# Moving the block merges and the two recurrences of a chunked DeltaNet layer, and putting three half projections between the last recurrence's steps

## The chip, the core and the metric

One core of a Trainium2 chip runs the whole program. The metric is the device time of one execution in microseconds (us), as the median of several runs. The profile shows one execution, with the work of every engine: PE is the matmul engine, DVE, ACT and POOL work on vectors, and SP issues the loads.

## The reference

Two decoder layers over 512 positions of width 1024, in float32. Layer 0 mixes tokens with a gated DeltaNet (8 heads of 128), layer 1 with a convolution module; each then attends to a memory of 256 rows and applies a squared-ReLU MLP. The change lies in the DeltaNet of layer 0 and at the seam to the attention behind it:

```python
proj = h @ w_in                       # q, k, v, z, and two gates for each head
qkv = silu(causal_depthwise_conv(qkv, w_conv))
# by chunk: (I + L) is unit lower triangular, L = strict(k_beta k^T * decay)
sol = triangular_solve(a_mat, rhs)    # u, w
def step(state, inp):                 # over the chunks, in order
    v_new = uc - wc @ state
    o = qd @ state + ai @ v_new
    state = state * exp(gl) + kd^T @ v_new
o = o * rsqrt(mean(o * o) + eps) * out_norm * silu(z)
h = h + o.reshape(B, S, 1024) @ w_out
```

## The kernel before

Activations are held transposed, as eight tiles of 128 channels by 512 positions. A weight tile and an activation tile are each split into a high and a low part (`wh`, `wl` and so on), and a product is three matmuls (`mm3`, lines 220 to 222). So a projection of one output tile is 24 matmuls, and half a projection, over four of the eight input tiles, is 12.

The weights of a unit are loaded by SP into one of three `raw` buffers (line 193), copied to `wh` by ACT (line 204) and subtracted to `wl` by DVE (line 72). Three pairs of `wh` and `wl` exist, and `wnext` asks for the splits of the next two units when a unit begins.

The DeltaNet works in chunks of 128 positions, four of them, and in two groups of four heads. Its order is written out by hand: `mains` is a list of units of PE work, most of them half a projection (`halves`), and `S.at(i, rank, f)` puts a side step behind unit `i`, the lower ranks first. Units 4 to 33 are the projections k, q, z and v of group 0, units 34 to 65 those of group 1, and units 66 to 81 the keys and values of the memory for the attention (`kv_unit`; the first eight give K, with 256 columns for each matmul, the last eight V). A scheduler then orders each engine's queue from that list, by priorities and by when it expects an operand; each engine works through its own queue strictly in that order.

The side steps that the change moves:

- The merge. The triangular matrix of each chunk is inverted in blocks of 32. DVE eliminates within the blocks (`fs_steps`, with tiles `FT`, `X`, `fst`) and ends with two transposes, to `TB` and `UB` (`fs_end`, lines 517 and 518, behind units 29 and 58). Then, for each head, `mg_a` copies four blocks of `TB` to `x` on ACT (line 537) and four of `UB` to `u` on POOL (line 538); `mg_w` multiplies (line 546) and copies to `w` (line 548); `mg_y`, three times, multiplies (line 558), copies to `y` (line 561) and adds to `u`. `MG` is the unit where this starts for each group; the second group's heads start up to two units before it.
- The recurrence. `rec(gq, c, step)`: for each chunk `c` three steps in three units. Step 0 multiplies keys and state (`kS`, line 618) and forms `r` on DVE; step 1 multiplies with the inverse (`vn`, line 630) and scales to `vnd` and `vn` on DVE; step 2 updates the state (`S`, line 641) and gives the outputs (`qS`, line 652, and `o`, line 658). `o_gate` follows in the third unit behind, and `o_norm` (root on ACT at line 680, scaling of the four `z` tiles on POOL and DVE) one unit after the last gate. `REC` is the first unit for each group.
- `head_out` transposes a head's gated output (`ogT`, line 691) and splits it into `oh` and `ol` for the output projection `do`. Heads 0 to 3 are done at units `HO` = 76 to 79.
- `load_x` loads the residual input again, behind unit `REC[1] + 6`.

Other steps in these stretches: each conv head is evicted by DVE (`cv`, line 72), scaled by ACT (lines 415 and 419), added by POOL (`cva`) or DVE (line 75), and passed through Silu by ACT (line 426). `k2` and `q2` (lines 440 to 466) form the Gram products of a head. The memory's norm runs beside it: squares on ACT (line 710), sums on POOL (`msq`), a product on PE (`mssq`, line 719), the root on ACT, scaling on POOL (`mem`) and the split into `mh` and `ml` on ACT and DVE (`mem_gain`), which the K units read.

After the list, the output projection is written out: first halves of units 0 and 1 over heads 0 to 3, then `head_out` for heads 4 to 7, then the second halves, and units 2 to 7 whole. `do_ev` adds the residual and starts the attention's norm.

Of the kernel before, what the change touches and what calls it, by code (L numbers as in the profile page):

```python
# [40 lines left out]
def tile_trunk(ctx, tc, xT, memT, prm_d, adt_d, bdw_d, w_ab, w_kq, w_v, w_z, w_dno, w_pw1, w_pw2,  # L41
# [13 lines left out]
    def nm(s):  # L55
        cnt[0] += 1
        return f"{s}_{cnt[0]}"

    def slot(dt=F32, s="u", shape=(P, NT)):
        return up.tile(list(shape), dt, tag="u", name=nm(s))  # L60

    def psum(s="ps"):
        return psp.tile([P, NT], F32, tag="ps", name=nm(s))
# [7 lines left out]
    def tt(e, o, a, b, op):  # L71
        e.tensor_tensor(out=o, in0=a, in1=b, op=op)  # L72
# [24 lines left out]
    def load_x():  # L97
        r = []
        for t in range(KT):
            h = slot(s="x")  # L100
            nc.sync.dma_start(out=h, in_=xT[t * P:(t + 1) * P, :])
            r.append(h)
        return r
# [84 lines left out]
    def wload():  # L188
        u = ws["load"]
        key, hf = order[u]  # L190
        ws["load"] += 1
        raw = wp.tile([P, 1024], F32, tag="raw", name=nm("raw"), bufs=NRAW)
        nc.sync.dma_start(out=raw, in_=srcs[key][:, hf * 1024:(hf + 1) * 1024])
        ws["raw"][u] = raw

    def wsplit():
        u = ws["split"]
        ws["split"] += 1
        while ws["load"] <= u:
            wload()  # L200
        raw = ws["raw"].pop(u)
        h = wp.tile([P, 1024], F32R, tag="wh", name=nm("wh"), bufs=NW)
        lo = wp.tile([P, 1024], F32R, tag="wl", name=nm("wl"), bufs=NW)
        act.copy(h, raw)  # L204
        tt(dve, lo, raw, h.bitcast(F32), ALU.subtract)
        ws["hl"][u] = (h, lo)

    def wnext(key, hf):
        i = ws["next"]
        assert order[i] == (key, hf), (order[i], key, hf)  # L210
        while ws["load"] < min(i + NRAW + 2, len(order)):
            wload()
        while ws["split"] < min(i + (NW if i else 1), len(order)):
            wsplit()
        ws["next"] += 1
        return ws["hl"].pop(i)

    def mm3(ps, wk, xk, first, last):
        (wh, wl), (xh, xl) = wk, xk
        pe.matmul(ps, wh, xh, start=first, stop=False)  # L220
        pe.matmul(ps, wh, xl, start=False, stop=False)  # L221
        pe.matmul(ps, wl, xh, start=False, stop=last)  # L222

    def wk(w, k):
        c = slice(k * P, (k + 1) * P)
        return w[0][:, c], w[1][:, c]

    def proj(w, xs, ps, k0=0, k1=KT):
        for k in range(k0, k1):
            mm3(ps, wk(w, k), xs[k], k == 0, k == KT - 1)  # L230
# [31 lines left out]
    def run(mains, sides):  # L262

        last = max(int(k[0]) for k in sides) + 1
        for i in range(max(len(mains), last)):
            if i < len(mains):
                mains[i]()
            for k in sorted(k for k in sides if k[0] == i):
                for f in sides[k]:
                    f()  # L270
# [476 lines left out]
    def kv_unit(layer, u):  # L747
        if u == 0:
            KV[layer] = ([], {})
        K, V = KV[layer]  # L750
        if u < 8:
            if u % 2 == 0:
                mem["ps"] = psum("K")
            hf = u % 2
            proj(wnext(("K", layer, u // 2), hf), mem["xs"], mem["ps"][:, hf * 256:(hf + 1) * 256])
            if hf == 1:
                K.append(split(mem["ps"], "K"))
        else:
            v = u - 8
            g, q, hf = v // 4, v // 2 % 2, v % 2  # L760
            if v % 4 == 0:
                mem["ps"] = [psum("V") for _ in range(2)]
            proj_moving(wnext(("V", layer, g * 2 + q), hf), hf, q, mem["xs"], mem["ps"])
            if v % 4 == 3:
                for mt in range(2):
                    V[mt, g] = split(mem["ps"][mt], "V")
# [338 lines left out]
    mains, S = [], Sides()  # L1105
# [27 lines left out]
    for u in range(16):  # L1133
        mains.append(lambda u=u: kv_unit(0, u))

    def squares(t0, t1):
        for t in range(t0, t1):
            n0.square(xin[t])

    S.at(0, 0, squares, 0, SQ0)  # L1140
    S.at(0, 3, wsplit)
    S.at(0, 2, squares, SQ0, 8)
    S.at(T_STAT, 0, n0.stat)
    S.at(T_STAT + 2, 0, n0.spread)
# [20 lines left out]
    for gq in range(2):  # L1165
# [6 lines left out]
        for i in range(4):  # L1172
            h = 4 * gq + i
            m = MG[gq] + i * MSTEP[gq] // 2
            S.at(m, 1, D.mg_a, h)
# [6 lines left out]
        for c in range(4):  # L1182
            for step in range(3):
                S.at(REC[gq] + n, 0, D.rec, gq, c, step)
                n += 1
            S.at(REC[gq] + n, 5, D.o_gate, gq, c)
        S.at(REC[gq] + n + 1, 1, D.o_norm, gq)
    S.at(MEM, 7, mem_load)
# [2 lines left out]
    S.at(MEM + 9, 3, mem_stat)  # L1191
    S.at(at["kv"] - MGAIN, 6, mem_gain, 0, 0)
    S.at(at["kv"] - MGAIN + 1, 6, mem_gain, 0, 1)
    os_, xres = [], []
    for i in range(4):
        S.at(HO + i, 6, lambda i=i: os_.append(D.head_out(i)))
    S.at(REC[1] + 6, 8, lambda: xres.extend(load_x()))
    run(mains, S)
# [4 lines left out]
    def do_ev(m, ps):  # L1203
        hn = slot(s="h")
        tt(dve, hn, ps, xres[m], ALU.add)
        h.append(hn)
        n1.add(m, hn)

    def do_w(m):
        return wnext(("do", m // 2), m % 2), psum("do")  # L1210

    w0, p0 = do_w(0)
    proj(w0, os_, p0, 0, 4)
    w1, p1 = do_w(1)
    proj(w1, os_, p1, 0, 4)
    for i in range(4, 8):
        os_.append(D.head_out(i))
    proj(w0, os_, p0, 4, 8)
    do_ev(0, p0)
    proj(w1, os_, p1, 4, 8)  # L1220
    do_ev(1, p1)
    for m in range(2, 8):
        w, ps = do_w(m)
        proj(w, os_, ps)
        do_ev(m, ps)
    n2 = Norm("mlp_norm0")
    h = xattn(0, n1, h, n2)
# [85 lines left out]
Q2 = (16, 18, 20, 21, 46, 48, 48, 51)  # L1313
FS = ((20, 9), (50, 8))
MSTEP = (0, -1)
MG = (32, 63)
V2 = (4, 3)
MGAIN = 4
HO = 76
REC = (39, 68)  # L1320
MEM = 53
MLP_ORDER = [("up", 0), ("up", 1), ("dn", 0), ("up", 2), ("dn", 1), ("up", 3), ("dn", 2), ("dn", 3)]
TAP_RATE = 1.5
# [95 lines left out]
```

## Time and profile before

| | us |
|---|---|
| median of 3 runs (1599.11 to 1601.5) | 1600.11 |
| the profiled execution | 1601.85 |
| its span, from first to last instruction | 1599.7 |
| PE busy | 1542.7 |
| DVE busy | 924.3 |
| ACT busy | 660.6 |
| POOL busy | 275.9 |

The mean granted clock of PE is 0.983. PE's busy time is 96% of the span. The DeltaNet ends at some 380 us; the rest of the span is attention, MLP and the second layer. A queue's wait is seen in the idle time in front of an instruction: the profile gives it in brackets, with the instruction that ended it.

### The profile page before, as it was taken

How to read it: one execution, taken by the hardware profiler on the slowest of the kernel's cores; microseconds unless marked ns; L12 is line 12 of the kernel's file. 1: busy time of each engine (PE TensorE's matmuls, PEld its weight loads, DVE VectorE, ACT ScalarE, POOL GpSimd, SP SyncE). 2: the span in 40 equal slices, each digit the busy share in tenths (PEclk: the TensorE clock that was granted, in tenths of full speed). 3: DMA queues.
4: the chain of work that ended last, by engine and by line, in shares of the span. 5: the costliest groups of instructions: out<-in, count | busy, mean ns of one | idle time of the engine just before them, and what ended most of it. 6: DMA issues, size and time to landing. Idle time of an engine off the chain costs nothing.

```text
span 1599.7 us, 20039 instructions
## 1 busy us (share of the span) xinstructions
PE 1542.7 (96%) x7864; PEld 1307.5 (82%) x7864; DVE 924.3 (58%) x1373; ACT 660.6 (41%) x1011; POOL 275.9 (17%) x314
## 2 busy tenths in 40 slices
PE   9998997899999999999999999799999999999997
PEld 6777885798888888888888889788888888888897
DVE  6886878576455444343436599974545443444443
ACT  6656573745444433232314321173434442322332
POOL 1526334502111100000111308102012000000002
PEclk9999999899999999999999999899999999999999
DMA  5221112153211232232232421253213222322321
GB/s 178 67 72 60 53 51 95 53 172 110 94 63 64 92 105 93 94 104 92 94 104 93 141 90 47 85 160 106 79 40 99 95 97 92 105 93 93 104 93 53
DMA packets 47614, 147.09 MB, mean 92 GB/s; under 512 B 6304, under 2 KB 11040, under 8 KB 47520
## 3 DMA queue, kind: packets, MB, share of 16 engines
q1 hardware_dynamic: 47520, 145.81, 27.6%
q8 instruction: 62, 1.02, 0.3%
q14 instruction: 32, 0.26, 0.1%
HBM read 142.38 MB, written 2.10 MB: 90 GB/s over the span
## 4 chain that ended last, share of the span: by engine, by line
PE 89%; DVE 3%; POOL 3%; ACT 2%; issue 1%; DMA 0%; DVEq 0%; SPq 0%; POOLq 0%; ACTq 0%
PE dn L222 7%; PE dn L220 7%; PE dn L221 7%; PE up L220 7%; PE up L222 7%; PE up L221 7%; PE pw L220 3%; PE pw L221 3%; PE pw L222 3%; PE q L220 2%; PE xo L221 2%; PE q L221 2%; PE q L222 2%; PE cv L1024 2%; PE xo L220 2%; PE xo L222 2%
## 5 line engine op out<-in xcount | busy, mean ns | idle before, releaser
L204 ACT CAST wh<-raw 128x1024 fp32r<-128x1024 f32 x248 | 260.5, 1051 | 717.5 <-PE dn L221 191.4
L72 DVE TENSOR_TENSOR wl<-raw,wh 128x1024 fp32r<-128x1024 f32 x248 | 314.2, 1268 | 127.4 <-ACT wh L204 121.5
L220 PE MATMUL up<-xh,wh 128*128 128x512 f32 x512 | 200.2, 391 | 0.0
L222 PE MATMUL up<-xh,wl 128*128 128x512 f32 x512 | 199.2, 389 | 0.0
L221 PE MATMUL up<-xl,wh 128*128 128x512 f32 x512 | 199.2, 389 | 0.0
L220 PE MATMUL dn<-uh,wh 128*128 128x512 f32 x448 | 174.3, 389 | 0.0
L221 PE MATMUL dn<-ul,wh 128*128 128x512 f32 x448 | 174.3, 389 | 0.0
L222 PE MATMUL dn<-uh,wl 128*128 128x512 f32 x448 | 174.3, 389 | 0.0
L72 DVE TENSOR_TENSOR h<-dn,h 128x512 f32<-128x512 f32 x56 | 41.8, 747 | 170.4 <-PE dn L222 170.4
L75 DVE SCALAR_TENSOR_TENSOR rl<-up,rb 128x512 f32<-128x512 f32 x64 | 44.2, 691 | 156.9 <-PE up L222 156.9
L221 PEld LDWEIGHTS up<-xl,wh 128*128 128x128 f32 x512 | 96.1, 188 | 20.3 <-issue 0.5
L220 PEld LDWEIGHTS up<-xh,wh 128*128 128x128 f32 x512 | 96.1, 188 | 20.1 <-issue 0.5
L222 PEld LDWEIGHTS up<-xh,wl 128*128 128x128 f32 x512 | 96.1, 188 | 20.1
L72 POOL TENSOR_TENSOR tap<-ident,prm 128x512 f32<-128x512 f32 x45 | 61.0, 1388 | 278.6 <-PE up L222 263.8
L221 PEld LDWEIGHTS dn<-ul,wh 128*128 128x128 f32 x448 | 84.1, 188 | 17.6
L222 PEld LDWEIGHTS dn<-uh,wl 128*128 128x128 f32 x448 | 84.1, 188 | 17.5
L220 PEld LDWEIGHTS dn<-uh,wh 128*128 128x128 f32 x448 | 84.1, 188 | 17.3
L72 POOL TENSOR_TENSOR sq<-sq,sq 128x512 f32<-128x512 f32 x30 | 49.9, 1664 | 255.4 <-ACT sq L295 167.7
L75 DVE SCALAR_TENSOR_TENSOR ca<-xg,prm,ca 128x384 f32<-128x384 f32 (+3 forms) x159 | 88.2, 607 | 0.3
L220 PE MATMUL h<-xh,wh 128*128 128x512 f32 x192 | 77.5, 403 | 1.3 <-ACT xh L288 1.3
L221 PE MATMUL h<-xl,wh 128*128 128x512 f32 x192 | 75.5, 393 | 0.6 <-DVE xl L75 0.6
L222 PE MATMUL h<-xh,wl 128*128 128x512 f32 x192 | 75.2, 392 | 0.0
(320 smaller groups left out, 3204.4 us busy)
## 6 DMA issues: line engine op xcount, KB each, us to landing
raw<-w_up SPq DMA_DIRECT2D x64, 512.0 KB, 3.5
raw<-w_dn SPq DMA_DIRECT2D x64, 512.0 KB, 3.5
raw<-w_pw SPq DMA_DIRECT2D x24, 512.0 KB, 3.7
raw<-w_kq SPq DMA_DIRECT2D x16, 512.0 KB, 3.6
raw<-w_k SPq DMA_DIRECT2D x16, 512.0 KB, 3.7
raw<-w_vv SPq DMA_DIRECT2D x16, 512.0 KB, 4.0
raw<-w_q SPq DMA_DIRECT2D x16, 512.0 KB, 3.6
raw<-w_o SPq DMA_DIRECT2D x16, 512.0 KB, 3.6
```

Of the source, the lines that this page charges most:

```text
L72: e.tensor_tensor(out=o, in0=a, in1=b, op=op)
L75: dve.scalar_tensor_tensor(out=o, in0=a, scalar=s, in1=b, op0=op0, op1=op1)
L204: act.copy(h, raw)
L220: pe.matmul(ps, wh, xh, start=first, stop=False)
L221: pe.matmul(ps, wh, xl, start=False, stop=False)
L222: pe.matmul(ps, wl, xh, start=False, stop=last)
L1024: pe.matmul(o, x, TAPS[m][2 * j + u // 4][:, (u % 4) * P:(u % 4 + 1) * P], start=u == 0, stop=False)
```

## The change

The merges start two and three units later (`MG`), the recurrences two and four (`REC`), and with `REC[1]` also `load_x`. The first halves of the output projection's units 0, 1 and 2 become units 82 to 84 of the list, so that the last steps of the second recurrence stand between them; the list's end moves with the last gate and `o_norm`. Afterwards the second halves of these three units follow on `head_out` of heads 4 to 7.

```diff
+    os_, xres, first = [], [], []
+
+    def do_first(m):
+        first.append((wnext(("do", m // 2), m % 2), psum("do")))
+        proj(first[m][0], os_, first[m][1], 0, 4)
+
+    for m in range(NDO):
+        mains.append(lambda m=m: do_first(m))
...
-    def do_w(m):
-        return wnext(("do", m // 2), m % 2), psum("do")
-
-    w0, p0 = do_w(0)
-    proj(w0, os_, p0, 0, 4)
-    w1, p1 = do_w(1)
-    proj(w1, os_, p1, 0, 4)
     for i in range(4, 8):
         os_.append(D.head_out(i))
-    proj(w0, os_, p0, 4, 8)
-    do_ev(0, p0)
-    proj(w1, os_, p1, 4, 8)
-    do_ev(1, p1)
-    for m in range(2, 8):
-        w, ps = do_w(m)
-        proj(w, os_, ps)
+    for m in range(8):
+        if m < NDO:
+            w, ps = first[m]
+        else:
+            w, ps = wnext(("do", m // 2), m % 2), psum("do")
+        proj(w, os_, ps, 4 if m < NDO else 0, 8)
         do_ev(m, ps)
...
-MG = (32, 63)
+MG = (34, 66)
...
-REC = (39, 68)
+NDO = 3
+REC = (41, 72)
```

More of the change, by code (lines that the diff above doesn't have):

```diff
@@ L1193, in tile_trunk @@
     S.at(at["kv"] - MGAIN + 1, 6, mem_gain, 0, 1)
-    os_, xres = [], []
     for i in range(4):
```

## The prediction

> **What bounds the kernel now.** I read the page first, then the waits of PE up to 420 us, then the timelines of ACT, POOL and DVE around the two longest waits and the end of the second recurrence.
>
> The page's busy row of PE, in 40 slices of 40 us, with the granted clock:
>
> ```profile
> PE   9998997899999999999999999799999999999997
> PEclk9999999899999999999999999899999999999999
> ```
>
> PE is full nearly everywhere; the dips lie in slices 4, 7 and 8, in the DeltaNet, which is where the change acts. After 380 us PE is full, so what PE loses or gains before that arrives at the end undiminished. Who made PE wait up to 420 us (total, times, longest, us):
>
> ```profile
> PE mg L546 <- POOL msq L72: 11.2, 1, 11.2
> PE mg L546 <- ACT x L537: 6.1, 4, 4.9
> PE mg L558 <- POOL xg L969: 3.3, 1, 3.3
> PE ai L466 <- ACT cva L426: 1.9, 1, 1.9
> ```
>
> Both large ones are merges (`mg`). The first merge on ACT and POOL (start, us, engine, operation):
>
> ```profile
> 135.71 6.75 ACT L537 COPY x<-TB 32x128 f32<-32x128 f32 x16
> 143.59 0.63 ACT L426 ACTIVATE cva<-cva 128x512 f32<-128x512 f32 x1 [1.13 <-POOL cva L72]
> 145.61 0.74 ACT L415 ACTIVATE cva<-cv,prm 128x512 f32<-128x512 f32 x1
> 146.22 1.96 ACT L419 ACTIVATE cvq<-cv,prm 128x512 f32<-128x512 f32 x3
> ...
> 142.30 1.26 POOL L72 TENSOR_TENSOR cva<-cva,cvq 128x512 f32<-128x512 f32 x1
> ```
>
> The sixteen copies of the inverted blocks (`x`) run at once after the transpose; the Silu behind them waits for POOL's add that ends at 143.56. PE stands from 132.0 to 137.1, does the sixteen `mg` products at the copies' pace and starts its next projection at 143.76. The second merge:
>
> ```profile
> 278.12 0.63 ACT L426 ACTIVATE cva<-cva 128x512 f32<-128x512 f32 x1 [5.11 <-POOL cva L72]
> 278.39 1.25 POOL L72 TENSOR_TENSOR msq<-msq,msq 128x512 f32<-128x512 f32 x1
> 284.75 3.99 POOL L72 TENSOR_TENSOR cva<-cva,cvq 128x512 f32<-128x512 f32 x3
> 290.47 5.35 POOL L72 TENSOR_TENSOR mem<-mem,mrs 128x512 f32<-128x512 f32 x4 [1.66 <-DVE mrs L723]
> ```
>
> POOL does block copies (0.41 each), convolution adds and the memory norm in one queue, and ACT waits for its adds. The last step of the second recurrence up to the transposes for the output heads 4 to 7:
>
> ```profile
> 365.02 1.06 PE L658 MATMUL o<-vn,dt 128*128 128x128 f32 x8
> 371.69 0.22 ACT L680 ACTIVATE sm<-sm 128x16 f32<-128x16 f32 x1
> 372.27 4.53 POOL L72 TENSOR_TENSOR z<-z,sm 128x512 f32<-128x512 f32 x3 [30.22 <-DVE sm L682]
> 377.29 1.91 PE L691 MATMUL ogT<-ident,z 128*128 128x128 f32 x16
> ```
>
> From the end of `o` (366.0, where the next matmul starts) to POOL's last scaling (376.8) are 10.8 us. 24 matmuls of V and the 24 of two first halves, 48 x 0.227 = 10.9 us, hide it exactly.
>
> **What the change does, part by part.** The amount of arithmetic is the same, so only waits count. I followed each engine's built order of both kernels and put the durations above on it, by hand. A projection unit is 24 matmuls at 0.227 us, 5.45 us; a K unit 24 at 0.12, 2.87 us.
>
> *First merge (MG 32 to 34).* PE's sixteen L546 products now stand behind one more projection unit, so PE works to 137.5 instead of 132.0. POOL's queue is unchanged row for row: its last of three adds still ends at 143.56. ACT's queue is not: the sixteen copies are now behind the Silu that waits for that add and behind the next convolution's four scalings. Silu 143.59, then 0.54 + 0.61 + 1.84 us (pitches of those rows) gives 146.6 for the first copy, 153.3 for the end of the last (6.7 us). Before, the next projection started 1.3 us behind the last copy (142.46 to 143.76); so 154.6, which is 10.85 us later, with 5.45 us more done: **+5.4**. What follows (the Y products, transposes, halves) stays dense, as the copies that they wait for are 0.4 us each and lie behind half units.
>
> *First recurrence (REC 39 to 41).* In 163 to 268 us PE waited 1.0, 0.9 and 1.9 us, for r, vn and a Silu behind POOL. Two units later the same steps meet the same evictions. If all three waits go it is -3.8; if the Silu's grows, by the queue of ACT (table load 1.28, four block copies 1.7, a gate's square 0.6 ahead of it), about +3. DVE's substitution chain, which ends at the transpose for the second merge (TB at 270.6), begins its steps earlier on DVE's queue but then has one more `vn` (0.6) in it. I take **-1**, from walking these rows; ends -4 and +4.
>
> *Second merge (MG 63 to 66).* PE's order is now: v6, the memory's sum of squares (mssq), v7, first L546, 29 matmuls of K, L546, and so on. Before, L546 stood ahead of mssq; mssq waits for POOL's last msq add, which has kept its place behind the copies and adds, so PE still stands from 268.3 to 279.7. mssq to 281.6 (1.97), v7 to 287.1. The four copies for the first L546 are split on ACT by the memory's work. ACT: two table loads and the root 1.28 + 0.48 + 1.28, 284.7; wait for POOL's adds, 288.7; Silu and a cast, 290.4; memory scalings (0.91) and three copies, 292.6; scalings, four convolution scalings, two more pairs of memory scalings (which need POOL's mem rows, 294.2), 297.9; fourth copy 298.35. So PE stands a second time, 287.1 to 298.4. Then L546 1.1, K 29 (ten at 0.21 as after the gap of before, at 305.1, the rest 0.12) 4.4, two L546, one K and Y 2.9, K 18 2.15, L546 1.0, Y 2.0, transposes 2.0: 313.9 with two K units done; six more are 17.2 and the last Y between them 3.8: 334.9 for all eight and the merge. Before: two K units and the merge at 315.56, and six of 2.87, 332.8. **+2.1**; ends -4 (the memory scalings do not split the copies) and +6.
>
> *Second recurrence (REC 68 to 72) and the three first halves.* Its steps now lie between V units of 2.72 us and the three halves of 2.72 us; before they had K units of 2.87 and V halves of 2.72, with no wait of PE from 320 to 377, so I take 0 there (a late S or r costs up to 2). The halves' inputs (heads 0 to 3) stay ready. x's eight loads pass two weight loads on SP's queue and are then ahead of the third half's weights; before, they passed between 340 and 350 us at 318 GB/s with PE full: 0, at most 3.
>
> *The end.* Only the third half, 2.72 us, lies between the last `o` and the transposes. The chain after `o`, from the rows: add, gate, square, reduce and scalar 3.4 us as before to 369.4; then table load and root without the weight cast between, reciprocal, 370.0; POOL's three scalings 1.5 each. With o ending at T: first column ready T+5.2, third T+8.2; sixteen transposes 1.8, of which half before; first split head (0.7) T+9.2. PE has 2.72 + 1.8 us of work in these 9.2: **+4.7**, and I add 1 for a slow clock behind it. Bounds 3.5 (POOL faster) and 7.
>
> That slow clock is in the trace: PE waits 3.2 us at 83.3, and the nine z matmuls after 88.2 come 0.43 us apart instead of 0.23, 2.0 us lost. But at 143.76, after the first merge's sparse products, they come at 0.23. The Trainium skill ("TensorE: Matmul & The Clock Gate", the section on why this matters for your kernels) says that idle gaps over about 3 us between bursts should be avoided, since the array then falls back to half rate for some 3.4 us. By that rule alone each new gap would cost about 1.7 us more as an estimate; the trace agrees at 83 us and not at 143.
>
> **Sum.** 5.4 - 1 + 2.1 + 5.7 = +12.2 us. The profiled execution took 1601.85 us (span 1599.7); the median is 1.7 lower, 1600.11, and the difference goes on that: **1612.3**. By the ends of all terms: about +1 to +27.
>
> **Rivals.**
> *The slip is swallowed by the second merge's wait.* If DVE's chain to TB kept its absolute time, the 5.4 us would go into the 11.4 us that PE stands there: 1607. Against it: DVE idles 12.9 us before 149 and the chain's input comes from PE's Gram products. Chance 0.08.
> *Faster: the copies come before PE needs them.* The mechanism is the cover alone: if the Silu on ACT were released early, the copies would end at 142.5 as before and PE save a full unit, -5.45, and at the second merge PE would not stand after v7, 11.3 us less, 2.1 - 11.3 = -9.2. With the end's 5.7 and -1: -9.95, 1590.2. It decides where the first copy starts 5.4 us earlier than 146.6. Against it: POOL's add ends at 143.56 in a queue that starts at 135.7 with the transpose and has no hole. For it: POOL's spans are rough. Chance 0.07.
> *A slow clock after every gap.* First merge, second merge and end each lose 2 us on full units: 1612.3 + 5, as 1 is in the sum already, 1617.3. For it the 83 us rows, against it 143.76. Chance 0.12. The Trainium skill's rule above would be this case.
> *It does not do what it says.* The halves do stand between the steps in PE's order; the merges move by one unit on PE and not at all on POOL, which is in the sum. If the halves brought no wait at the end (POOL's scalings hidden): 1607, chance 0.05.
>
> **Numbers.** Forecast 0.68, rivals 0.32. Its own range is 1606 to 1620; with part of the rivals 1604 to 1622. No change means within 0.2%, 3.2 us, about what a measurement of this kernel can tell. Faster 0.07 is the one rival; the same 0.07, where low ends meet; slower 0.86.
>
> **What would show it.** Right: PE idle some 11 us ahead of the first L546 with the sixteen copies starting about 11 us after the transpose; two gaps of some 11 us at the second merge, with v7 between; some 5 us of holes around the last sixteen transposes; PE full from the eighth K unit to the last `o`. Wrong: the copies directly after the transpose, or no gap after v7, or the last transposes right behind the third half.

## The result, and the profile after

The changed kernel is slower by 18.3 us: a median of 1619.11 us (1618.18 to 1620.24, 4 runs) against 1600.80 for the kernel before on the same chip (1599.11 to 1603.68, 4 runs), a ratio of 1.011 with a 95% interval of 1.0095 to 1.0125. The forecast was 1612.3, with a range of 1604 to 1622. The profiled execution took 1619.25 us, with a span of 1617.6 (17.9 more than before); the mean granted clock is 0.977 (0.983 before).

The page's row of PE and the granted clock, 40 slices of 40.4 us:

```profile
PE   9997989699999999999999999799999999999997
PEclk9997999799999999999999999899999999999999
```

PE dips in slices 4, 6 and 8 (4, 7 and 8 before). Slices 4 and 8 are deeper than before, the new one in slice 6 is a wait in the first recurrence, and the long wait of the second merge has moved from slice 7 to slice 8. Who made PE wait up to 440 us (total, times, longest, us):

```profile
PE mg L546 <- ACT x L537: 15.2, 3, 11.4
PE mssq L719 <- POOL msq L72: 11.2, 1, 11.2
PE ai L466 <- ACT cva L426: 5.9, 1, 5.9
...
PE ogT L691 <- POOL z L72: 3.2, 3, 2.5
```

The wait for the memory's sum of squares is as long as before, 11.2 us, now ahead of `mssq` itself. The copies `x` cost 15.2 us (6.1 before), the `ai` product 5.9 (1.9 before), and the last transposes 3.2, where there was none.

The first merge, on ACT, POOL and PE (start, us, engine, operation; in brackets the idle time in front and what ended it):

```profile
135.71 1.04 ACT L204 CAST wh<-raw 128x1024 fp32r<-128x1024 f32 x1
144.59 0.63 ACT L426 ACTIVATE cva<-cva 128x512 f32<-128x512 f32 x1 [7.84 <-POOL cva L72]
...
147.58 6.76 ACT L537 COPY x<-TB 32x128 f32<-32x128 f32 x16
...
143.31 1.25 POOL L72 TENSOR_TENSOR cva<-cva,cvq 128x512 f32<-128x512 f32 x1
...
148.95 7.13 PE L546 MATMUL mg<-x,bt 128*128 128x96 f32 x32 [11.38 <-ACT x L537]
```

At 135.7, where the copies ran before, ACT now casts one weight and then stands 7.8 us at a Silu for POOL's third add. The copies start 11.9 us later than before, and PE stands 11.4 us for them. The Trainium skill ("Perfetto Trace Analysis", per-engine timelines) says that ACT, DVE and GPSIMD work strictly first in, first out; the trace agrees, as TB had been ready since about 135 and the copies still waited behind the Silu.

The first recurrence, where the prediction went wrong, on ACT and PE. In the kernel before:

```profile
216.30 1.74 ACT L493 COPY DB<-bt 32x128 f32<-32x128 f32 x4 [0.93 <-POOL bt L72]
...
221.73 0.63 ACT L426 ACTIVATE cva<-cva 128x512 f32<-128x512 f32 x1
...
222.41 1.16 PE L466 MATMUL ai<-cva,cva 128*128 128x128 f32 x8 [1.92 <-ACT cva L426]
```

In the changed kernel:

```profile
219.16 1.73 ACT L493 COPY DB<-bt 32x128 f32<-32x128 f32 x4 [2.96 <-POOL bt L72]
...
223.38 1.28 ACT L575 ACT_TABLE_LOAD   x1
...
225.32 1.69 ACT L493 COPY DB<-bt 32x128 f32<-32x128 f32 x4
...
228.67 0.63 ACT L426 ACTIVATE cva<-cva 128x512 f32<-128x512 f32 x1
...
229.35 2.08 PE L466 MATMUL ai<-cva,cva 128*128 128x128 f32 x8 [5.90 <-ACT cva L426]
```

ACT again stands for POOL (3.0 us, at the first block copy), then has eight block copies, two table loads and a root ahead of the Silu that PE needs. Before, it stood 0.9 us at that copy, and three of the eight copies came behind the Silu. ACT is not alone in being late: the Silu's own input is the last of DVE's sums for that head, which ends at 227.34, just when ACT is through with the copies; these sums wait for an add on POOL in their turn.

The second merge and the end, on PE:

```profile
291.17 2.08 PE L719 MATMUL mssq<-msq,ones 128*128 128x256 f32 x4 [11.23 <-POOL msq L72]
...
303.84 1.89 PE L546 MATMUL mg<-x,bt 128*128 128x96 f32 x8 [3.23 <-ACT x L537]
...
396.87 0.66 PE L691 MATMUL ogT<-ident,z 128*128 128x128 f32 x4 [2.49 <-POOL z L72]
```

The gap after v7 is 3.2 us, not 11. The transposes begin 5.5 us behind the end of the last `o` (391.4), 2.5 of them uncovered. The sixteen then take 3.2 us, from 396.87 to 400.08, as they wait for POOL between them; before, they took 1.7 (377.29 to 378.95). To split the slip I read, in both traces, when PE reaches the same piece of work:

| point on PE | before | after | slip | of it in this stretch |
|---|---|---|---|---|
| first `dt` product after the first merge (three units and the merge done) | 168.47 | 175.53 | 7.1 | first merge +7.1 |
| first unit of the value heads, group 1 | 252.01 | 263.46 | 11.45 | first recurrence +4.4 |
| end of the eighth K unit (before: 315.56 with two done, and six of 2.87) | 332.8 | 347.0 | 14.2 | second merge +2.7 |
| end of the third first half (before: the second ends at 377.45, and 2.72 for a third) | 380.17 | 394.38 | 14.2 | second recurrence 0.0 |
| end of the output projection | 417.62 | 435.88 | 18.3 | the end +4.1 |

The span grew by 17.9; the 0.4 are regained later. These are figures of one execution of each kernel, and the first merge differs between executions: by the same points it cost 5.6 us in the traces of two kernels that are tried below with the same late merge (only the first merge late, and `REC[1]` = 71).

### The profile page after: what moved, and what is told of

Read it like the earlier page. It is cut to its first block, busy times and chain, and to the rows that moved or that the text cites. A ratio compares the mean times of both kernels' runs of the same rounds, so it can differ in the third digit from the quotient of the medians.

```text
span 1617.6 us, 20036 instructions
## 1 busy us (share of the span) xinstructions
PE 1548.2 (96%) x7864; PEld 1310.6 (81%) x7864; DVE 925.5 (57%) x1373; ACT 661.2 (41%) x1011; POOL 276.2 (17%) x314
## 4 chain that ended last, share of the span: by engine, by line
PE 83%; DVE 6%; POOL 4%; issue 4%; ACT 3%; DMA 0%; DVEq 0%; SPq 0%; POOLq 0%; ACTq 0%
PE dn L222 7%; PE dn L221 7%; PE dn L220 7%; PE up L220 7%; PE up L222 7%; PE up L221 7%; PE pw L220 3%; PE pw L221 3%; PE pw L222 3%; PE q L220 2%; PE xo L221 2%; PE q L221 2%; PE q L222 2%; PE cv L1024 2%; PE xo L220 2%
```

## The experiments

Each is timed in turn with the kernel before on its own chip, and its difference is to that median, which was between 1600.8 and 1603.1. The changed kernel stands at +18.3 in this measure.

| kernel | median | difference to before | ratio (95%) |
|---|---|---|---|
| only the first merge late | 1608.88 | +6.6 | 1.0042 (1.0029 to 1.0054) |
| only the first recurrence late | 1608.46 | +6.2 | 1.0041 (1.0028 to 1.0054) |
| only the second group and the halves | 1607.62 | +5.3 | 1.0037 (1.0025 to 1.0049) |
| change, copies early | 1616.22 | +13.9 | 1.0090 (1.0077 to 1.0103) |
| change, value heads 2 and 3 by DVE | 1611.90 | +10.4 | 1.0070 (1.0056 to 1.0083) |
| first recurrence late, `ai` later | 1603.76 | +2.2 | 1.0019 (1.0010 to 1.0028) |
| first recurrence late, no POOL ahead | 1604.23 | +2.5 | 1.0016 (1.0007 to 1.0025) |
| change, memory early | 1622.39 | +20.8 | 1.0131 (1.0116 to 1.0146) |
| change, `REC[1]` = 71 | 1616.17 | +14.6 | 1.0100 (1.0086 to 1.0115) |
| change, value heads by DVE, memory early | 1605.24 | +2.2 | 1.0012 (1.0003 to 1.0020) |
| before, value heads by DVE, memory early | 1593.92 | -9.2 | 0.9951 (0.9935 to 0.9966) |
| the same, `MG[0]` = 34 with early copies | 1590.55 | -12.5 | 0.9923 (0.9910 to 0.9935) |

### The change in three parts

```diff
 # the kernel before
-MG = (32, 63)
+MG = (34, 63)
```

> The kernel before, with MG[0] = 34 alone: only the first group's merge is two units later. Theory A (each part of the change costs on its own, and the 5.9 us for which PE waits at the ai product of the second group's last head but one belongs to the recurrence's new place): the merge alone costs what the trace of the changed kernel shows for it, +7.1 us, so 1607.9 against 1600.8, and the ai wait stays at about 1.9. Theory B (the late merge pushes the convolution chain of ACT and POOL out of step for good, and the ai wait follows from that): +11.5 us, 1612.3, with an ai wait near 6. Both: a gap of PE of 11.4 us ahead of the first L546, with the sixteen copies behind the Silu on ACT.

Measured +6.6 us, the 11.4 us gap at the first merge and an `ai` wait of 1.9: theory A. (The profiled execution lies 2.9 us above this kernel's median, so the median is taken. Its span is 10.4 us longer than before: 5.6 by the first merge, and 4.8 by a slow clock behind that `ai` wait, which the last section shows.)

```diff
 # the kernel before
-REC = (39, 68)
+REC = (41, 68)
```

> The kernel before, with REC[0] = 41 alone: only the first group's recurrence is two units later. Theory A (the ai wait belongs to the recurrence's new place, as its table load, root and block copies on ACT now stand ahead of that Silu): +4.4 us, 1605.2, with an ai wait near 6. Theory B (it follows from the late merge): about 0, 1600.8, with an ai wait near 1.9. The prediction's own term for this part was -1, 1599.8. The first merge stays as before, a gap of 4.9 us.

Measured +6.2 us, with an `ai` wait of 5.9 and the first merge as before (4.9). So the recurrence's new place brings this wait by itself; the forecast of -1 is refuted. The size is 1.8 above what the stages of the changed kernel's trace gave, 4.4, which lies just under the interval (4.5 to 8.7). This kernel's own trace agrees with the smaller figure: from the first `dt` product to `mssq` it takes 117.5 us, and the kernel before 113.0, so 4.5.

```diff
 # the changed kernel
-MG = (34, 66)
+MG = (32, 66)
-REC = (41, 72)
+REC = (39, 72)
```

> The changed kernel with MG[0] = 32 and REC[0] = 39: the first group as before, the second group's merge and recurrence and the three halves as in the change. If the parts add up: 2.7 for the second merge, 0.9 in the second recurrence and 3.2 at the end by the trace of the changed kernel, +6.8 us, 1607.6. The prediction's own terms for these parts give 2.1 + 0 + 5.7 = +7.8, 1608.6. If the first group's slip changes how the second merge falls (its wait for the memory's sums is a meeting of PE with POOL), the difference to 1607.6 is over 2 us either way.

Measured +5.3 us (4.0 to 7.9), with waits as in the changed kernel: 11.2 at `mssq`, 4.2 at the first product of the second merge, 2.8 at the last transposes. The three parts add up to 6.6 + 6.2 + 5.3 = 18.1, against 18.3 for the change. Each is known to some 2 us; within that they are independent: nothing of the slip of the first group is swallowed by the 11.2 us at the second merge, which are as long in all four kernels.

### The first merge: ACT behind POOL

```diff
 # the changed kernel
-            S.at(m, 1, D.mg_a, h)
+            S.at(m - MA[gq], 1, D.mg_a, h)
...
 MG = (34, 66)
+MA = (2, 0)
```

> The changed kernel, with the copies of the inverted blocks for the first merge (mg_a, lines 537 and 538) issued two units earlier than its products, where they stood before the change; on ACT they then stand ahead of the Silu that waits for POOL's add, and PE's order is that of the changed kernel. Theory A (the copies' place in ACT's queue is the whole cost of the first merge): the copies run from 135.7 to 142.5 us, PE restarts its projections at 143.8 instead of 155.8 with one unit more done than in the kernel before, so -12.0 us against the changed kernel, 1607.1. Theory B (the merge is bound by something else too: the products, POOL's copies of u, or the gain is waited away at the ai product or at the memory's sums): less than 6 us gained, 1613 or more.

Measured 4.4 us less than the change (13.9 for 18.3), not 12: theory B. The copies did run at 135.7, and PE had its sixteen products done at 143.2. It then stood elsewhere:

```profile
154.30 4.29 PE L558 MATMUL mg<-u,w 128*96 128x96 f32 x32 [8.13 <-ACT w L548]
...
143.78 0.63 ACT L426 ACTIVATE cva<-cva 128x512 f32<-128x512 f32 x1 [1.22 <-POOL cva L72]
...
153.15 0.63 ACT L426 ACTIVATE cva<-cva 128x512 f32<-128x512 f32 x1 [5.35 <-POOL cv L411]
153.68 1.61 ACT L548 ACTIVATE w<-mg 128x384 f32<-128x384 f32 x4
```

The copies of `w` for the next products are now behind the next head's Silu, which waits for POOL in its turn (its three adds end at 153.1; the profile names the small fill behind them). My theory A named the place in ACT's queue as the whole cause; it is the wait at the Silu, and whatever of the merge is behind it pays. So the next kernel takes that wait away, and leaves the copies where the change has them:

```diff
 # the changed kernel
-            self.VT[h] = self.conv_head(self.ps.pop(("v", h)), 16 + h, CONV_V)
+            self.VT[h] = self.conv_head(self.ps.pop(("v", h)), 16 + h, 0 if h in (2, 3) else CONV_V)
```

> The changed kernel, with the convolution sums of the value heads 2 and 3 made by DVE (line 75) and not by ACT and POOL; the sums themselves are the same up to rounding. Nothing else is edited, but the order on ACT follows: the Silu no longer waits for POOL's adds. Theory A (at the first merge ACT stands in its queue at a Silu that waits for POOL, and whatever of the merge is behind it, the copies of x or those of w, waits with it): without that wait the copies end near 144, PE restarts at about 145 instead of 155.8, no wait at the first Y products, so -10 us, 1609. Theory B (the merge's chain is long in itself: transpose, copies, products, w, Y): 3 us or less, 1616 or more, with the 8 us at the Y products again.

Measured 8.0 us less than the change: theory A, somewhat short of -10. PE restarts its projections at 146.0 (155.8 in the change) and does not wait at the first Y products; but the twelve matmuls from 146.0 come at 0.43 us, half rate, until 150.7 (stretch, its length, busy time and instructions of PE, PEld, DVE, ACT and POOL, granted clock, DMA share, GB/s):

```profile
146.00:150.80 4.80, 4.80 (x14) 3.79 (x14) 3.61 (x4) 2.41 (x7) 2.48 (x8) 0.52 0.29 109
```

At the first `dt` product it is at 167.24 (168.47 in the kernel before), so of the 7.1 us that the late merge cost nothing is left. The edit does two things at once: it takes POOL's adds out of the chain, and with them three of the four scalings of each head off ACT, 1.9 us for three. What each of the two gives was not tried apart; the wait for POOL was the longer, 7.8 us.

### The first recurrence

```diff
 # the kernel before with REC[0] = 41
-Q2 = (16, 18, 20, 21, 46, 48, 48, 51)
+Q2 = (16, 18, 20, 21, 46, 48, 50, 51)
```

> The kernel before with REC[0] = 41 as above, and the Gram product of head 6 with its query (ai) two units later (Q2[6] = 50 for 48), behind a z half and a step of the recurrence. Theory A (the 5.9 us are PE standing in its own queue for a Silu that comes late on ACT, and nothing else needs that product soon): the wait goes, -5.9 us against the recurrence alone, so 1602.6. Theory B (DVE and the state of the recurrence are as late as the Silu, by POOL's and DVE's queues): the wait moves to the S or kS products behind it, and the time stays within 2 us, 1606.5 or more.

Measured 4.0 us less than the recurrence alone, between the two theories. The `ai` wait is gone, and PE stands 3.3 us at the state's products instead:

```profile
217.91 2.08 PE L641 MATMUL S<-vnd,kt 128*128 128x128 f32 x8 [3.26 <-DVE vnd L72]
...
216.50 0.75 DVE L75 SCALAR_TENSOR_TENSOR cva<-cv,prm,cva 128x512 f32<-128x512 f32 x1 [2.26 <-POOL cva L72]
217.17 0.68 DVE L72 TENSOR_TENSOR vnd<-vn,sdec_neg 128x512 f32<-128x512 f32 x1
```

DVE's `vnd` stands behind a convolution sum that waits for POOL's add, as the Silu does on ACT. The last run takes POOL out of that chain:

```diff
 # the kernel before with REC[0] = 41
-            self.M["q", h] = self.conv_head(self.ps.pop(("q", h)), h, CONV_Q)
+            self.M["q", h] = self.conv_head(self.ps.pop(("q", h)), h, 0 if h == 6 else CONV_Q)
...
-            tt(pool, c4(bt0), c4(bt0), over_i(self.s_all[:, hc]), ALU.mult)
+            tt(dve if h in (6, 7) else pool, c4(bt0), c4(bt0), over_i(self.s_all[:, hc]), ALU.mult)
```

> The kernel before with REC[0] = 41 as above, with POOL taken out of the chain ahead of that Silu: DVE scales the Gram matrices of heads 6 and 7 (bt times s_all) and makes the convolution sum of query head 6. Theory A (of the 5.9 us wait, the part that comes from ACT standing 3.0 us for POOL's scaling of bt is all that POOL explains; the two table loads, the eight block copies and the root stay ahead of the Silu): by those rows the Silu starts some 2.5 to 3 us earlier, the ai wait falls to about 3, and the time to about 3 us below the recurrence alone. Theory B (POOL explains nearly all of it): the wait falls under 1 us, 5 us or more gained. Theory C (DVE, with 2.5 us more work, is as late): no gain.

Measured 3.7 us less, with an `ai` wait of 3.7: nearest to theory A. POOL explains about 2.2 us of the 5.9; the rest are block copies, two table loads and DVE's own queue ahead of the Silu. The traces do not bear out the whole 3.7: from the first `dt` product to `mssq` this kernel takes 116.2 us, 1.3 less than with the recurrence alone, as two waits at `vn` (1.6 for 0.7) give part back. The other 2.4 lie within the noise of the two medians.

### The second merge

```diff
 # the changed kernel
-MEM = 53
+MEM = 50
```

> The changed kernel with the memory's norm three units earlier (MEM = 50 for 53): loads, squares, sums and scalings. The sums are then done before the second merge. Theory A (PE's 11.2 us ahead of mssq come from msq standing in POOL's queue behind block copies and adds): that wait goes, and ACT has fewer items ahead of the copies: 6 to 11 us gained, 1608 to 1613. Theory B (ACT and POOL are full in this stretch, 30 and 28 of 47 us, and the K units and the second merge's copies need their results at the same time as before): the wait comes back at K or at the second L546, 4 us gained or less, 1615 or more.

Measured 2.5 us more than the change: theory B. The gain of theory A is out; that this kernel is slower than the change is not shown, as the two intervals overlap. The wait at `mssq` fell to 3.1 and came back, longer, at the K unit (PE's waits, then ACT and POOL):

```profile
PE K L220 <- ACT mh L741: 13.4, 2, 12.6
...
PE mssq L719 <- POOL msq L72: 3.1, 1, 3.1
```

```profile
299.83 0.63 ACT L426 ACTIVATE cva<-cva 128x512 f32<-128x512 f32 x1 [7.54 <-POOL cva L72]
...
284.09 5.91 POOL L538 COPY u<-UB 32x128 f32<-32x128 f32 x13 [11.00 <-DVE UB L518]
...
291.22 4.91 POOL L72 TENSOR_TENSOR mem<-mem,mrs 128x512 f32<-128x512 f32 x4
296.10 4.91 POOL L72 TENSOR_TENSOR cva<-cva,cvq 128x512 f32<-128x512 f32 x4
```

ACT has no more to do than before, it stands 7.5 us (and 3.3 at the next Silu) for POOL's adds, which are behind copies and the memory's scaling. `mh`, which K reads, is behind these Silus. So POOL is the queue to shorten. With the sums of the value heads 2 to 7 by DVE (the edit above with `h in (2, 3, 4, 5, 6, 7)`) and `MEM = 50`:

> The changed kernel with the convolution sums of the value heads 2 to 7 made by DVE, and the memory's norm three units earlier (MEM = 50). POOL then has only its block copies and the scaling of the memory in the second merge. Theory A (both merges of the changed kernel are bound by POOL's queue, reached by way of ACT, which stands in its own queue for POOL's adds): 7.2 us as measured with heads 2 and 3 alone, and at the second merge the waits at mssq (11.2), at the first L546 (3.2) and at K's products (1.2) go, with the slow clock behind them; 13 to 17 us more than heads 2 and 3 alone: 1595 to 1599, which is below the kernel before. Theory B (with the memory early alone the wait only moved to K, so the second merge is bound by the length of ACT's work): 1608 or more.

Measured 16.1 us less than the change and 8.2 less than with heads 2 and 3 alone: the direction of theory A, but not its size (13 to 17). The waits at `mssq` (11.2) and the first L546 (3.2) fell to 3.1 and 1.9, but K still stands 5.2 us for `mh`, as POOL's sixteen block copies took 9.8 us and its scaling of the memory 5.6 behind them. The `ai` wait of 5.9 and the 3.2 at the last transposes are still in it. So it stays just slower than the kernel before (0.5 to 3.2 us).

### The end

```diff
 # the changed kernel
-REC = (41, 72)
+REC = (41, 71)
```

> The changed kernel with REC[1] = 71 for 72: two first halves, and not one, lie between the last o and the transposes of heads 4 to 7; the rest of PE's order is nearly the same. Theory A (the end's cost is POOL's scaling of z without cover): 2.5 of the 3.2 us of waits at these transposes go, 1616.6. Theory B (the slow clock behind that gap costs as much as the gap): 4 us or more go, 1615. Theory C (the end costs nothing, its waits are hidden by something later): no change, 1619.1.

Measured 3.7 us less than the change. The waits at the transposes fell from 3.2 to 1.0, and 1.5 of the rest were there at `mssq` already (289.67 for 291.17), where both kernels have the same order. Theory A; B's slow clock does not show, as the granted clock behind the gap is 1.00 in the changed kernel (below). C is out by the trace, where the waits fell; the two medians alone would not show it, as their intervals overlap.

### Without POOL in the chain, from the kernel before

> The kernel before with the same two edits: sums of value heads 2 to 7 by DVE, MEM = 50. Theory A (POOL's queue is what PE stands for at the second merge of the kernel before as well): the 11.2 us ahead of mssq go, the copies of the second merge then wait for DVE's transpose at 270.6 and some 5 us of that show: about -8, 1593. The first merge gains nothing, as its copies come directly after the transpose already. Theory B (the wait moves to K or to the copies in full): 1600 or more.

> The same, and the first merge's products two units later (MG[0] = 34), with its copies issued where they stood before. Theory A (a later merge is worth its cover once ACT no longer waits for POOL): PE no longer stands 4.9 us for the transpose and its copies at the first merge, 3 to 5 us below the kernel without this edit. Theory B (what is gained there is given back in the Y products or the slow clock behind sparse products): within 2 us of it.

The first (sums of value heads 2 to 7 by DVE, `MEM = 50`) measured 9.2 us less than the kernel before; the second, with `MG[0]` = 34 and the copies at their old place, 12.5 less: theory A in both, and 3.4 us for the later merge. The sums by DVE and the early memory were not tried apart on this kernel. In the second no wait of PE over 5 us is left up to 440 us: the longest around the merges are 4.2 at the second one's Y products, 3.4 at its first product, and 2.9 at `mssq`. A later merge is worth its cover, but only once ACT doesn't stand for POOL. This version is faster than both kernels, against the one before by 0.8%.

## Why the prediction was right, and where not

The sign and the range held; the forecast difference was 6.1 us short, 12.2 for 18.3. One step, the first recurrence, was wrong by 5.4 us and in its sign; the other terms were off by less, and in part they cancel, which is luck.

- **First merge, +5.4: right in its mechanism, 1.7 short.** The copies did go behind the Silu and its wait for POOL, and PE stood 11.4 us ("some 11"). POOL's third add ended at 144.56, not at 143.56, so everything came 1.2 later (restart at 155.8 for 154.6), and the first twelve matmuls behind lost 0.7 to a slow clock. In the two other traces with this merge, at 5.6 us, the projections behind it run at full rate, so the term itself was nearly exact, and 1.5 of the 7.1 belong to the clock of this one execution. Shown alone: +6.6.
- **First recurrence, -1: the step that failed.** The prediction named the queue of ACT (table load, block copies, square) as a possible loss of "about +3", then took the gain of the small waits instead. The Silu's wait grew from 1.9 to 5.9; +4.4 in the trace, +6.2 alone (4.5 in that kernel's trace). Of the 4.4, 4.0 are the longer wait, 1.5 a slow clock behind it (`ai` and `S` take 3.3 us from 229.3, at a granted clock of 0.55, for 1.8 at full rate), and 1.1 of the other small waits are gained. This one term makes up most of the miss.
- **Second merge, +2.1: the sum right (2.7), its parts not.** The gap after `mssq` came as said. The second one was 3.2 us for 11.3, since I took the first product to need four copies: line 546 reads columns 0 to 95 of `x`, so three of the four blocks, and these stand ahead of the scalings that split off the fourth. Against that, v7 took 7.9 us for 5.45 and the 29 matmuls of K 9.2 for 4.4, at about half clock and with three waits of 0.41 for `ml`. The one error covered the other, so that the sum is right by luck.
- **Second recurrence, 0: right.** PE has no wait from 347 to 394 us; x's loads brought none.
- **The end, +5.7: the mechanism right, 1.6 too much.** POOL's scalings of `z` came 1.0 us apart, not 1.5, and the clock behind stayed full, so the 1 us for it was not due: 4.1, of which 3.2 are the waits at the transposes.
- **The rivals.** The slip was not swallowed by the second merge's wait: that is 11.2 us in every kernel where the memory kept its place. "Copies before PE needs them" did not happen by itself, but the experiments made it so, and that is the faster version. "A slow clock after every gap" holds at two of the three places, for 0.7 us at the first merge and several at the second, and at a fourth, the first recurrence. The prediction's evidence against it was misread. In the kernel before, the clock did fall behind the gap of 4.9 us at the first merge (columns as in the stretch shown above):

```profile
137.00:143.70 6.70, 6.59 (x31) 6.62 (x32) 0.00 (x0) 5.38 (x14) 6.13 (x12) 0.51 0.01 2
```

The half rate fell on the sparse merge products, whose pace the copies set, and was over when the projections restarted at 143.76.

## What to carry to other kernels

An engine that stands in its queue for another holds up all that is behind it, whoever needs it: when steps are moved, ask of each queue what is now ahead of the moved step and for whom that waits, and don't count on a cover of one unit. A wait that is only moved shows up at the next reader of the same queue (copies, then `w`; `mssq`, then K; `ai`, then `vnd`), so look for the queue that is waited for last, here POOL's, and shorten that. And count the operands that an instruction really reads before pricing its wait.

## What the hardware showed that was not expected

The same sum costs much less on DVE than on POOL, and needs one scaling on ACT less for each tap; the form's rows in the changed kernel between 120 and 330 us (min, median and max in ns):

```profile
L72 POOL TENSOR_TENSOR cva<-cva,cvq x27: 1252/1291/2252, 119.9 to 319.3; 128x512 f32<-128x512 f32 x27
L75 DVE SCALAR_TENSOR_TENSOR cva<-cv,prm,cva x20: 739/752/1664, 157.3 to 238.7; 128x512 f32<-128x512 f32 x20
```

The Trainium skill ("GPSIMD Engine Reference", 4.1, engine selection) gives elementwise work to the vector engine, as GPSIMD is about 2 times slower with two inputs; the trace agrees in the main, with 1.7 times here, 1.29 for 0.75 us.

The granted clock after PE's gaps (stretch, its length, busy time and instructions of PE, PEld, DVE, ACT and POOL, granted clock, DMA share, GB/s):

```profile
155.79:159.30 3.51, 3.51 (x15) 2.83 (x15) 1.95 (x3) 2.37 (x4) 0.00 (x0) 0.79 0.00 0
291.10:300.60 9.50, 9.43 (x28) 7.30 (x28) 1.75 (x1) 4.32 (x6) 8.70 (x18) 0.68 0.01 2
303.80:314.40 10.60, 9.25 (x37) 8.08 (x38) 8.30 (x10) 9.00 (x20) 6.73 (x6) 0.52 0.15 49
400.00:408.00 8.00, 7.92 (x34) 6.39 (x35) 6.60 (x9) 5.68 (x9) 0.00 (x0) 1.00 0.11 34
```

A gap of 2.5 us cost no clock (the last row); behind one of 3.2 us, which followed a unit that had begun at half rate itself, 10.6 us came at 0.52. The Trainium skill's rule on the clock, cited in the prediction, separates these two gaps rightly at about 3 us. But no such limit holds over all traces of this case. In the kernel with only the first merge late, PE waited 1.9 us at `ai`, and soon behind it, with PE busy throughout, 10 us came at half rate:

```profile
229.50:239.50 10.00, 10.00 (x38) 8.89 (x37) 6.29 (x11) 3.36 (x8) 1.80 (x4) 0.51 0.15 53
```

In the kernel before, the same product waited 1.9 us too, and the clock stayed at 1.00. That half rate lasts only some 3.4 us, as the prediction took from the Trainium skill, is not what these two stretches show either. So half rate can come behind a short wait, in one execution and not in another; what decides that, and what ends it, was not tried.
